# A planner that supposes a somewhat longer time for each fp32r matmul: a two-layer gated diffusion block on one core

## The chip, the core and the metric

The kernel runs on one core of a Trainium2 chip. The metric is the device time of one execution in microseconds (us), as a median of runs. A core has a matrix engine (TensorE, PE in the profile, with its weight loads as PEld), a vector engine (VectorE, DVE), a scalar engine (ScalarE, ACT), GpSimd (POOL) and SyncE (SP), which issues the DMA transfers here. Each engine takes its instructions in program order, and waits where an operand or a buffer is not ready.

## The reference, cut to what matters

512 latent tokens and 256 context tokens of width 1024 pass two layers (`DEPTH = 2`). In each layer the tokens are normed and modulated, projected to many parts by `w_in`, and go through four branches (a differential attention with 4 heads, a latent attention with 8 heads, a pooling mixer, a convolution); the branches are gated and merged, and a squared-ReLU MLP follows. In the second layer only the latent tokens are still needed behind the attention's keys and values.

```python
for l in range(DEPTH):
    px = split_in(modulate(rmsnorm(x, g_norm1[l]), mod_x[0], mod_x[1]) @ w_in[l])
    pc = split_in(modulate(rmsnorm(xc, g_norm1[l]), mod_c[0], mod_c[1]) @ w_in[l])
    ...
    ya_x = diff_post(attend(qa_x, ka_all, va_all, coef_a), g_sub_a[l], lam_init)
    yb_x = from_heads(attend(qb_x[None], kb_all[None], vb_all, coef_b))
    mix_x = merge_branches([ya_x, yb_x, pool_mixer(...), conv_mixer(...)],
                           px[10], w_branch[l], w_o[l])
    x = x + mod_x[2] * mix_x
    x = x + mod_x[5] * squared_relu_mlp(modulate(rmsnorm(x, g_norm2[l]), mod_x[3], mod_x[4]),
                                        w_ff1[l], w_ff2[l])
```

## The kernel before

**Arithmetic.** Every fp32 operand of a large product is split into a high and a low part of type fp32r (ACT makes the high part, DVE the low one), and each product is three matmuls: high x high, high x low, low x high. A weight block arrives by DMA in a raw buffer (`wr`), ACT writes `wh`, DVE writes `wl`, and PE multiplies into a PSUM tile (`mm`, and in the second layer's MLP also `mp`, `sp`, `pp`). Transposes through PE and a few true fp32 matmuls are the rest of PE's work.

**Stages.** For each layer: an attention stage (projections, both attentions, and beside them units of the gates, the pooling and the convolution), a merge stage, and an MLP stage. The second layer's MLP uses a seven-product scheme for part of its blocks.

**Who sets the order.** The program is not issued as it is written. Every instruction is recorded by `Plan.rec` with a cost from `Plan.cost`, into streams: B (the main line), A (an attention head), F (fill units: gates, pooling, convolution) and M (modulation work for later). `Plan.flush` gives each instruction of a stage a key: its stream's share of PE cost done so far, stretched over the whole stage's PE cost (M goes by DVE cost). `Plan.order` is a list scheduler: it simulates the five engines with these costs and with fixed hand-over times, and lets each engine take, of the instructions that are ready at its simulated time, the one with the lowest key. `Plan.replay` then emits the instructions in order of their simulated start, and pins that order per engine. Buffers of most kinds are handed out in recorded order, so the recorded order matters as well. It is set in part by `do_fill`, which is called at 37 places in layer 0 and 41 in layer 1 and records fill units of a list of 52 per layer for as long as the part of them recorded is below the part of the main line's PE cost `m / MAINPE[l]`.

The lines that matter in what follows:

```python
            if meth == 'transpose':
                return 109.0 if n > 64 else 60.0
            if ins[0].dtype == F32R:
                return n / 2.4 + 3 if n >= 256 else 4 * n / 2.4
...
            c = 0.833 * n + (52 if psum else 94)
...
                    lat = 0.0 if eng == 'SP' else (362.0 if je == 'PE' else 200.0 if je == 'ACT' or eng == 'PE' else 152.0)
...
            while fill and (nfill - len(fill)) < nfill * (m / MAINPE[l]):
```

They are the planner's charges for a PE transpose, for an fp32r matmul with n moving columns, for an ACT instruction with n columns, the hand-over time from one engine to another (`je` is the engine that waits), and the gate for fill units.

Of the kernel before, what the change touches and what calls it, by code (L numbers as in the profile page):

```python
# [33 lines left out]
HOLD = 0.85  # L34
TOG = (1, 0, 2, 1, 1)
FFLEAD = {'M': (0.1, 0.8)}
MAINPE = (327313, 279633)


class _Rec:  # L40
# [11 lines left out]
class Plan:  # L52
# [22 lines left out]
    def rec(self, eng, fn, meth, a, k):  # L75
        i = len(self.ops)
        ap0 = k['out'] if 'out' in k else a[0]
        outs = [ap0] + ([k['accum_out']] if k.get('accum_out') is not None else [])
        ins = [x for x in a[(0 if 'out' in k else 1):] if isinstance(x, bass.AP)]
        ins += [v for n, v in k.items() if n not in ('out', 'accum_out') and isinstance(v, bass.AP)]  # L80
        cost = self.cost(eng, meth, outs[0], ins, k)
        if eng == 'PE':
            self.pe += cost
        self.ops.append([eng, fn, a, k, cost, outs, ins])
        self.keys.append(0.0)
        self.phase.append(self.nphase)
        self.phase_ops.setdefault(self.stream, []).append(i)
# [30 lines left out]
    def cost(self, eng, meth, out, ins, k):  # L118
        n = self.free(out)
        if eng == 'PE':  # L120
            if meth == 'transpose':
                return 109.0 if n > 64 else 60.0
            if ins[0].dtype == F32R:
                return n / 2.4 + 3 if n >= 256 else 4 * n / 2.4
            return max(1000.0, 4 * n / 2.4)
        if eng == 'ACT':
            psum = any(x.space == bass.MemoryType.PSUM for x in ins[:1])
            c = 0.833 * n + (52 if psum else 94)
            c += 93.0 * (len(ins) - 1) + (93.0 if k.get('accum_out') is not None else 0)
            return c  # L130
        if eng == 'DVE':
            psum = any(x.space == bass.MemoryType.PSUM for x in ins) or out.space == bass.MemoryType.PSUM
            if meth == 'tensor_reduce':
                return 1.04 * self.free(ins[0]) + 69
            if meth == 'reciprocal':
                return 6.4 * n + 69
            if meth == 'tensor_tensor':
                return 1.04 * n + 69
            if meth == 'scalar_tensor_tensor':
                return 1.04 * n + 69 + 60 * (len(ins) - 2)  # L140
            return (1.04 if psum else 0.52) * n + 69 + 60 * (len(ins) - 1)
        if eng == 'POOL':
            return 1.0 * n + 80
        return 500.0
# [18 lines left out]
    def order(self):  # L163
# [3 lines left out]
        acc = {}  # L167
        tiles = {}
        for i, (eng, fn, a, k, cost, outs, ins) in enumerate(ops):
            touched = set()  # L170
            for w, aps in ((0, ins), (1, outs)):
# [55 lines left out]
        for i, (eng, fn, a, k, cost, outs, ins) in enumerate(ops):  # L227
            s = set(ap.tensor.name for ap in outs + ins if hasattr(ap.tensor, 'tag'))
            optiles[i] = [x for x in s if tiles[x][0] is not None]
# [134 lines left out]
def tile_block(ctx, tc, xT, ccol, wmod, cols, rows, wqkv, wcq, wckv, wuq, wukv, wpool,  # L364
# [825 lines left out]
    for l in range(DEPTH):  # L1190
# [30 lines left out]
        def do_fill():  # L1221
# [3 lines left out]
            s_, plan.stream = plan.stream, 'F'  # L1225
            while fill and (nfill - len(fill)) < nfill * (m / MAINPE[l]):
                fill.pop(0)()
# [398 lines left out]
```

## Time and profile before

| what | value |
|---|---|
| time before, median of 3 runs | 2667.26 us (2666.79 to 2670.55) |
| time of the profiled execution | 2668.45 us |
| span of the profiled execution (first to last instruction) | 2666.7 us |
| granted TensorE clock, mean | 0.999 of full |
| PE busy | 2630.7 us, 99% of the span |
| PEld busy | 2314.4 us, 87% |
| DVE busy | 1850.4 us, 69% |
| ACT busy | 1201.0 us, 45% |

Times in the rows are microseconds from the span's start; the mean of one instruction is in ns. A matmul's record reaches past the start of the next one, since matmuls are pipelined; how often one starts is read from the starts, not from the length of a record. All instructions carry line 352, since one helper emits them: groups are told apart by the names of their tiles.

### The profile page before, as it was taken

Reading aid. Unit: us, or ns where it says so; the run is one execution under the profiler, and the core shown is the slowest. Engines: PE = TensorE matmul, PEld = TensorE weight load, DVE = VectorE, ACT = ScalarE, POOL = GpSimd, SP = SyncE. Lnnn points to the kernel's source line nnn. Section 1 sums busy time; section 2 is a strip of 40 time slices with the busy share of each in tenths; the row PEclk is TensorE's granted clock in tenths of the full one; section 3 lists DMA queues with packets and bytes.
Section 4 is the critical chain, followed back from the end, with each engine's and each line's share of the span. In section 5 each row is a group of like instructions: output and inputs, shape, how many; then the busy total and the mean of one; then the engine's idle time right before and its main releaser. Section 6 shows DMA issues by size and latency. Waiting matters only on the chain.

```text
span 2666.7 us, 43004 instructions
## 1 busy us (share of the span) xinstructions
PE 2630.7 (99%) x15988; PEld 2314.4 (87%) x15988; DVE 1850.4 (69%) x4174; ACT 1201.0 (45%) x2488; POOL 13.7 (1%) x63
## 2 busy tenths in 40 slices
PE   8999999999999999999999999999999999999999
PEld 4898889988998888988888888888888888999988
DVE  6678666689986777445455467786467887887664
ACT  4355453445564135514141334555455562565443
POOL 0000000000000000000000000000000000000000
PEclk9999999999999999999999999999999999999999
DMA  7212233243446643333344323223232267433232
GB/s 246 77 62 70 85 109 114 94 125 118 129 135 198 216 134 105 103 97 109 114 136 127 121 95 100 68 68 106 93 98 83 90 182 225 149 109 107 84 103 95
DMA packets 189538, 311.97 MB, mean 117 GB/s; under 512 B 21520, under 2 KB 72080, under 8 KB 189328
## 3 DMA queue, kind: packets, MB, share of 16 engines
q1 hardware_dynamic: 189328, 309.22, 37.0%
q8 instruction: 126, 2.06, 0.3%
q14 instruction: 84, 0.69, 0.1%
HBM read 270.86 MB, written 38.27 MB: 116 GB/s over the span
## 4 chain that ended last, share of the span: by engine, by line
PE 92%; DMA 3%; DVE 3%; ACT 2%; issue 1%; SPq 0%; ACTq 0%; DVEq 0%
PE mm L352 75%; PE pst L352 8%; PE sc L352 5%; PE pp L352 2%; PE sp L352 1%; PE mp L352 1%; DMA wmp<-in_wmod_dram 1%; ACT wh L352 1%; DMA wr<-in_wff_dram 0%; DVE wl L352 0%; DMA wr<-in_wqkv_dram 0%; DMA gt<-g 0%; DMA wr<-in_wckv_dram 0%; DVE hl L352 0%; DVE e L352 0%
## 5 line engine op out<-in xcount | busy, mean ns | idle before, releaser
L352 ACT ACTIVATE wh<-wr 128x512 fp32r<-128x512 f32 (+3 forms) x616 | 367.1, 616 | 607.5 <-PE mm L352 453.4
L352 PE MATMUL mm<-hh,wh 128*128 128x512 f32 (+1 forms) x1792 | 539.5, 351 | 3.5 <-ACT gt L352 2.0
L352 PE MATMUL mm<-hh,wl 128*128 128x512 f32 (+1 forms) x1792 | 535.7, 349 | 0.8 <-DVE wl L352 0.8
L352 PE MATMUL mm<-hl,wh 128*128 128x512 f32 (+1 forms) x1792 | 533.1, 348 | 0.0
L352 DVE TENSOR_TENSOR wl<-wr,wh 128x512 fp32r<-128x512 f32 (+3 forms) x616 | 409.3, 673 | 132.4 <-ACT wh L352 118.6
L352 PEld LDWEIGHTS mm<-hh,wh 128*128 128x128 f32 x1792 | 333.9, 189 | 41.3 <-ACT gt L352 3.2
L352 PEld LDWEIGHTS mm<-hh,wl 128*128 128x128 f32 x1792 | 334.7, 189 | 39.5 <-DVE wl L352 1.1
L352 PEld LDWEIGHTS mm<-hl,wh 128*128 128x128 f32 x1792 | 334.1, 189 | 37.9
L352 DVE SCALAR_TENSOR_TENSOR macc<-wm,silu,macc 128x256 f32<-128x256 f32 x448 | 204.9, 479 | 96.2 <-DMA wm<-in_wmod_dram 90.2
L352 PE MATMUL mm<-ah,wh 128*128 128x512 f32 (+1 forms) x768 | 242.6, 356 | 0.4 <-ACT wh L352 0.3
L352 PE MATMUL mm<-al,wh 128*128 128x512 f32 (+1 forms) x768 | 242.1, 356 | 0.0
L352 PE MATMUL mm<-ah,wl 128*128 128x512 f32 (+1 forms) x768 | 241.7, 356 | 0.0
L352 ACT ACTIVATE ph<-pst 128x384 fp32r<-128x384 f32 (+1 forms) x216 | 102.9, 476 | 138.4 <-PE pst L352 136.6
L352 PEld LDWEIGHTS mm<-ah,wh 128*128 128x128 f32 x768 | 144.6, 188 | 22.1 <-ACT wh L352 0.8
L352 PEld LDWEIGHTS mm<-al,wh 128*128 128x128 f32 x768 | 144.6, 189 | 21.0 <-issue 0.2
L352 PEld LDWEIGHTS mm<-ah,wl 128*128 128x128 f32 x768 | 144.4, 188 | 21.1 <-issue 0.2
L352 ACT ACTIVATE e<-sc,st 128x768 f32<-128x768 f32 (+1 forms) x160 | 130.2, 814 | 67.5 <-DVE st L352 36.6
L352 PE MATMUL mm<-wh,hh 128*128 128x256 f32 x544 | 154.0, 287 | 2.2 <-ACT wh L352 1.1
L352 PE MATMUL mm<-wl,hh 128*128 128x256 f32 x544 | 155.0, 287 | 0.9 <-DVE wl L352 0.9
L352 PE MATMUL mm<-wh,hl 128*128 128x256 f32 x544 | 154.2, 285 | 0.0
L352 DVE SCALAR_TENSOR_TENSOR xx<-mm,mod,xx 128x256 f32<-128x256 f32 (+1 forms) x96 | 61.3, 659 | 133.8 <-PE mm L352 133.6
L352 DVE TENSOR_REDUCE st<-sc 128x1 f32<-128x768 f32 (+1 forms) x160 | 135.3, 846 | 20.6 <-PE sc L352 18.7
(233 smaller groups left out, 5112.6 us busy)
## 6 DMA issues: line engine op xcount, KB each, us to landing
wr<-in_wff_dram SPq DMA_DIRECT2D x280, 256.0 KB, 3.0
wr<-in_wdense_dram SPq DMA_DIRECT2D x192, 256.0 KB, 3.1
wm<-in_wmod_dram SPq DMA_DIRECT2D x320, 128.0 KB, 2.3
wr<-in_wbr_dram SPq DMA_DIRECT2D x64, 256.0 KB, 3.4
wr<-in_wqkv_dram SPq DMA_DIRECT2D x48, 256.0 KB, 2.8
g<-gt SPq DMA_DIRECT2D x32, 384.0 KB, 2.6
gt<-g SPq DMA_DIRECT2D x32, 384.0 KB, 3.5
wr<-in_wo_dram SPq DMA_DIRECT2D x48, 256.0 KB, 3.1
```

The costliest lines, as they stand in the source:

```text
L352: ins = fn(*a, **k).ins
```

## The change

Two constants of the planner change; no instruction is added, removed or resized. An fp32r matmul with 256 or more moving columns is charged n/2.4 + 13 ns in place of n/2.4 + 3 ns, and the two totals of main-line PE cost that the fill gate divides by are raised.

```diff
-MAINPE = (327313, 279633)
+MAINPE = (348900, 297430)
...
             if ins[0].dtype == F32R:
-                return n / 2.4 + 3 if n >= 256 else 4 * n / 2.4
+                return n / 2.4 + 13 if n >= 256 else 4 * n / 2.4
```

## Rows read from the trace of the kernel before

**Rows 1.** The page's first part: busy us (share of the span), instructions.

```profile
span 2666.7 us, 43004 instructions
...
PE 2630.7 (99%) x15988; PEld 2314.4 (87%) x15988; DVE 1850.4 (69%) x4174; ACT 1201.0 (45%) x2488; POOL 13.7 (1%) x63
```

**Rows 2.** Windows by time: busy us of each engine, clock, DMA share, GB/s.

```profile
500.00:900.00 400.00, 397.09 (x2533) 356.31 (x2532) 332.75 (x853) 202.29 (x457) 0.17 (x3) 1.00 0.47 148
900.00:1300.00 400.00, 398.17 (x2283) 347.81 (x2282) 234.12 (x443) 136.77 (x245) 0.00 (x0) 1.00 0.37 114
```

**Rows 3.** Timeline of PE in two stretches: start, us, instructions merged.

```profile
2404.63 0.39 PE L352 MATMUL mm<-ah,wl 128*128 128x512 f32 x1
...
2408.26 0.39 PE L352 MATMUL mm<-ah,wh 128*128 128x512 f32 x1
...
2600.47 1.60 PE L352 MATMUL sp<-t,wsf 128*128 128x256 f32 x12
2601.91 0.28 PE L352 MATMUL pp<-hh,wsf 128*128 128x256 f32 x1
```

**Rows 4.** PE groups that are not fp32r matmuls: form, count, busy us, mean ns.

```profile
L352 PE MATMUL pst<-ident,e 128*128 128x128 f32 x624 | 103.8, 273 | 1.1 <-DVE pl L352 0.8
...
L352 PE MATMUL pst<-ident,tmp 128*96 128x128 f32 (+1 forms) x318 | 57.3, 274 | 3.5 <-DVE ql L352 2.5 <-DVE ks L352 0.5 <-DVE nw L352 0.2
...
L352 PE MATMUL mm<-wmp,silu 128*2 128x512 f32 x64 | 30.4, 626 | 7.2 <-DMA wmp<-in_wmod_dram 7.2
...
L352 PE MATMUL pst<-ident,macc 128*128 128x128 f32 x128 | 22.0, 272 | 0.0
...
L352 PE MATMUL pst<-ident,ob 128*128 128x128 f32 x80 | 14.7, 273 | 0.0
...
L352 PE MATMUL R<-e,ones 128*128 128x256 f32 (+1 forms) x16 | 6.0, 467 | 0.9 <-DVE e L352 0.8
...
L352 PE MATMUL pss<-ident,ss 128*128 128x128 f32 x22 | 3.6, 277 | 0.9 <-DVE ss L352 0.9
...
L352 PE MATMUL pst<-ident,mrow 2*128 2x2 f32 x16 | 1.6, 202 | 1.6 <-ACT mrow L352 1.6
```

**Rows 5.** PE's waits in layer 0's attention stage (100 to 860): total, times, longest.

```profile
PE mm L352 <- ACT gt L352: 2.1, 3, 1.1
PE sc L352 <- ACT e L352: 1.2, 2, 0.7
PE pst L352 <- DVE pl L352: 0.8, 1, 0.8
PE pst L352 <- DVE ks L352: 0.5, 2, 0.4
```

**Rows 6.** PE's waits in layer 1's attention stage (1590 to 2170).

```profile
PE mm L352 <- ACT gt L352: 2.4, 3, 1.3
PE pst L352 <- DVE ql L352: 1.5, 3, 0.9
PE sc L352 <- ACT e L352: 1.2, 1, 1.2
PE mm L352 <- ACT wh L352: 1.1, 3, 0.7
PE mm L352 <- ACT wgh L352: 1.0, 1, 1.0
PE mm L352 <- DVE wl L352: 0.9, 1, 0.9
PE mm L352 <- DVE va L352: 0.5, 1, 0.5
PE pst L352 <- DVE nw L352: 0.2, 1, 0.2
```

**Rows 7.** The chain of work around one wait of PE, in order of time.

```profile
2368.05 0.53 ACT wsf L352
2368.58 0.04 issue
2368.63 0.50 PE sp L352 x2
```

**Rows 8.** All waits: the longest of ACT, and the weight split's form.

```profile
ACT wh L352 <- PE mm L352: 453.4, 163, 7.3
...
L352 ACT ACTIVATE wsf<-wr 128x512 fp32r<-128x512 f32 x84 | 51.1, 628 | 99.1 <-PE mm L352 50.5 <-issue 20.3 <-PE sp L352 8.6
```

## The prediction

> **What bounds the kernel now.** I read the page's totals first. The reader is to see that PE is busy for 2630.7 of 2666.7 us and DVE for 69% [rows 1]: all the time that PE stands idle is 2666.7 - 2630.7 = 36.0 us. The windows by time say the same of single stages: in a stretch of attention (500 to 900) PE is busy 397 of 400 us although DVE is at 333, and in a stretch of merge and MLP (900 to 1300) 398 of 400 with DVE at 234; the granted clock is full in both [rows 2]. So PE's own work sets the end, and an order of instructions can only move the waits between it.
>
> Next come PE's waits. In the two attention stages, where the order has most to choose, they are 2.1 + 1.2 + 0.8 + 0.5 = 4.6 us in 8 waits [rows 5] and 2.4 + 1.5 + 1.2 + 1.1 + 1.0 + 0.9 + 0.5 + 0.2 = 8.8 us in 14 [rows 6]: 13.4 us in 22 waits. Elsewhere the waits that one can name are fixed by data: 7.2 us for the first transfers, 1.6 us for `mrow`, 0.9 and 0.8 us in a norm [rows 4]. What is left, 36.0 - 13.4 - 10.5 = 12.1 us, is spread over stage borders and the end.
>
> A wait costs more than its idle time. A 256-column record is 0.28 us long, while the twelve of `sp` start every (2601.91 - 2600.47)/12 = 0.120 us [rows 3]; so about 0.28 - 0.12 = 0.16 us of each wait is hidden below the record before it. The 22 waits then cost 13.4 + 22 x 0.16 = 16.9 us, or 0.77 us each.
>
> **The change part by part.** *The charge.* Of 15988 matmul records [rows 1], 624 + 318 + 128 + 80 + 22 + 16 = 1188 are transposes and 64 + 16 = 80 true fp32 [rows 4]; 14720 are fp32r matmuls, all of 256 columns or more, so the planner now supposes 14720 x 10 ns = 147 us more of PE time. On the chip nothing is added: the same 14720 matmuls run at the same pace, so the direct cost is zero, and no cover is needed for that, since no instruction exists.
>
> Which charge is nearer the chip? 256 columns cost 256/2.4 + 3 = 109.7 ns before and 119.7 after, and the chip starts one every 120 ns [rows 3]. 512 columns cost 216.3 before and 226.3 after, and the sixteen steps from 2404.63 to 2408.26 give 226.9 ns [rows 3]. So the old planner ran PE 147 us ahead of the chip, and the new one runs with it. The Trainium skill says otherwise ("TensorE: Matmul & The Clock Gate", section "Back-to-back issue gap"): at the full clock an isolated matmul starts N/2.4 + 2.5 ns behind the one before, which is nearly the old charge. By that page 256 columns would take 109 ns; the trace has 120, and the measurement decides.
>
> *What that does to the order.* A PE clock that ran fast made ACT and DVE look slow beside it: the plan saw PE run dry at places where it does not, and put other streams' work there. It also left slack: for each matmul planned between a request and its answer, the chip gave 10 ns more than the plan thought. With the new charge the plan sees about 5.5% (147/2667) more room for every other engine, so it should find fewer dry places; against that, the slack goes. How much slack remains without it? The split `wsf` is charged 0.833 x 512 + 94 = 520 ns and the hand-over to PE 362, together 882; the chip needs 628 [rows 8] and about 50 ns from the end of ACT's record to PE's start (2368.63 - 2368.58) [rows 7], together 678. So 204 ns of slack per such hop stay in the plan whatever a matmul is charged.
>
> Keys move little, as a stream's progress is a share of its own PE cost; within a stream, transposes (charged 109 as before) lose a little weight against matmuls. What moves is which instructions are ready when an engine picks.
>
> *The gate.* Counted from the loops, the main line records 2196 fp32r matmuls in layer 0 and 1880 in layer 1, so `m` grows by 21960 and 18800 by its end; MAINPE grows by 21587 and 17797. The differences, 373 of 348900 (0.1%) and 1003 of 297430 (0.3%), are 52 x 0.001 = 0.06 and 52 x 0.003 = 0.18 of a fill unit. In the middle the 256-column projections, which come first, rise by 9% and the whole by 6.5%, so a unit that stood just under its step is recorded one call earlier; the recorded order is otherwise the old one. Both edits of the gate I cost at nothing: what hides it is PE's full queue (ACT waits 453.4 us for `mm` buffers [rows 8], not PE for ACT); with that cover gone, a unit a call early would cost one wait of 0.77 us.
>
> No row shows a wait of the new order. Below, the bound is that all 13.4 us of attention waits go with their hidden part: -16.9 us. Above, that they come twice: +16.9 us. Nearest are today's waits themselves, which a new order mostly moves. I take a fifth of 13.4 us as gain, 2.7 us, a judgement: more room, and slack that survives.
>
> **The sum.** Profiled execution 2668.45 us (span 2666.7 and 1.75 around it), which is 1.2 above the median 2667.26. Work 0, waits -2.7: 2665.75, and 2664.6 beside the median.
>
> **The rivals.** *Same (forecast).* Waits change places; within 0.2% (5.3 us, about what a measurement of this kernel can tell from no change). 2664.6 us; own range 2662 to 2672.5.
>
> *Faster.* The true charge removes most waits that the old plan made by its mistake: 9 to 17 us of attention waits and borders, 2667.3 - 10 = 2657 us. For it: 22 short waits, each of one to a few matmuls' length [rows 5, 6], are what a plan with a wrong clock leaves. Against it: 13.4 us is all there is, and part of it (the first `ks`, `ql`) hangs on chains without filler.
>
> *Slower.* The lost slack decides: a softmax's way over DVE and ACT back to PE is now planned to the nanosecond, and a producer that is late on the chip (a DMA behind `wr`, another instruction ahead of it on DVE, which is at 83% in 500 to 900 [rows 2]) stops PE at once, and behind it all of PE's queue. It decides from 5.3/0.77 = 7 more waits than the 22. At 11 more: 11 x 0.77 = +8.5 us, 2676 us; at 22 more, 2684. For it: DVE's load, and that the plan pins PE's order. Against it: the 204 ns per hop.
>
> *The skill's pace.* If 2.5 ns were right, the new plan would run PE 147 us behind the chip and PE would come to every answer early, which is the slower case at its full price, 2684 us. Rows 3 speak against it; 0.02, inside the slower chance.
>
> *Nothing happens at all*, the order being the same: with 147 us of shift in 2667 hardly possible, and inside "same".
>
> **How the numbers follow.** Faster 0.32, same 0.43, slower 0.25. Predicted 2664.6. The range runs from 2654 (some 13 us, most of the attention's waits, gone) to 2679 (15 more waits, 11.6 us); about 0.1 is left out on each side.
>
> **What would show it.** Right: the same 15988 PE records and PE busy time within some us of 2630.7 where waits no longer hide; 0.120 and 0.227 us paces as before; PE's idle time, 36.0 us, down by 1 to 4; another order in the attention stages and nearly the old one in the MLPs. Wrong: idle time on PE up by over 5 us with waits for `e`, `pl` or `st` in the attention stages (slack lost), or down by over 5 us there (the old clock had cost more); or a time that moves with the MLP stages, where I expect nothing.

## The result, and the profile after

The changed kernel takes 2688.93 us (median of 4 runs, 2687.51 to 2690.88) against 2667.03 us for the kernel before (4 runs): a ratio of 1.008, 95% interval 1.0062 to 1.0097. It is slower by 21.9 us, outside the predicted range. The profiled execution took 2690.17 us, with a span of 2688.4.

The page's first part, of the changed kernel (busy us, share of the span, instructions):

```profile
span 2688.4 us, 42996 instructions
...
PE 2642.2 (98%) x15988; PEld 2316.2 (86%) x15988; DVE 1846.3 (69%) x4174; ACT 1203.0 (45%) x2488; POOL 13.4 (0%) x63
```

The span is 21.7 us longer than before [rows 1]. The same 15988 matmuls ran, PE stood idle for 2688.4 - 2642.2 = 46.2 us in place of 36.0 (10.2 more), and the other 11.5 us lie inside PE's busy time (2642.2 against 2630.7). DVE and ACT did the same instructions in nearly the same time.

Where the 11.5 us sit can be counted from the start of every PE record in the two traces. Stops of PE (idle time before a record, however short) rise from 63 to 91. The record before a stop reaches some 0.17 us past the pace, so 28 more stops put 5.1 us into busy time. The other 6.4 us are steps that take longer than the pace without any idle time, half of them among the six steps behind a stop. Few of the longer steps have the signal (semaphore) that the matmul waits for come inside them: they account for 5.1 us, against 4.0 before. So these 6.4 us are not shown to be short waits for another engine; what they are stays open.

The Trainium skill ("Perfetto Trace Analysis", section "Identifying the Most-Contended Engine") says that matmul busy time is not a good measure of how close a kernel is to the chip's limit, and points to the busy share of the weight loads beside another measure. Here too PE's busy time misleads: PEld is busy 1.8 us longer than before, PE 11.5, for the same instructions.

The pace of PE did not change. Timeline of PE, changed kernel, in the second layer's MLP (31 steps between these two records):

```profile
2422.83 0.39 PE L352 MATMUL mm<-ah,wl 128*128 128x512 f32 x1
...
2429.86 0.39 PE L352 MATMUL mm<-ah,wh 128*128 128x512 f32 x1
```

(2429.86 - 2422.83)/31 = 0.2268 us for 512 columns, as before (0.2269, [rows 3]) and nowhere near the 0.216 of the old charge.

The windows by time, changed kernel (length, then busy us of PE, PEld, DVE, ACT, POOL, clock, DMA share, GB/s):

```profile
500.00:900.00 400.00, 391.80 (x2485) 348.89 (x2484) 328.28 (x850) 199.39 (x456) 0.16 (x3) 1.00 0.44 141
900.00:1300.00 400.00, 398.77 (x2290) 348.73 (x2289) 236.97 (x443) 137.77 (x244) 0.00 (x0) 1.00 0.38 117
```

The stretch in attention lost (391.8 us busy and 2485 matmuls, against 397.1 and 2533 in [rows 2]); the one in merge and MLP did not (398.8 against 398.2); the clock is full in both. Where each stage ends says it more exactly. The first `mm<-mh,wh` matmul, the first product with the merged tokens, marks the end of a layer's attention and of nearly all its merge; the last `mm<-ah,wh` matmul of 256 columns marks the end of layer 0's MLP. Timeline of PE, kernel before:

```profile
967.38 0.40 PE L352 MATMUL mm<-mh,wh 128*128 128x512 f32 x1
...
1585.42 0.28 PE L352 MATMUL mm<-ah,wh 128*128 128x256 f32 x1
...
2269.95 0.28 PE L352 MATMUL mm<-mh,wh 128*128 128x256 f32 x1
```

Timeline of PE, changed kernel:

```profile
984.58 0.40 PE L352 MATMUL mm<-mh,wh 128*128 128x512 f32 x1
...
1600.42 0.28 PE L352 MATMUL mm<-ah,wh 128*128 128x256 f32 x1
...
2288.07 0.28 PE L352 MATMUL mm<-mh,wh 128*128 128x256 f32 x1
```

The delay is 984.58 - 967.38 = 17.2 us after layer 0's attention and merge, 1600.42 - 1585.42 = 15.0 after its MLP, 2288.07 - 2269.95 = 18.1 after layer 1's attention and merge, and 21.7 at the end. So layer 0's attention and merge carry most of it, layer 0's MLP wins back 2.2 us, layer 1's attention and merge lose 3.1, and the last MLP 3.6.

PE's waits in layer 0's attention stage, changed kernel, 100 to 870 (total us, times, longest):

```profile
PE pst L352 <- DVE pl L352: 3.7, 4, 1.4
PE pst L352 <- DVE e L352: 2.5, 2, 1.5
PE pst L352 <- DVE nw L352: 1.6, 1, 1.6
PE mm L352 <- ACT wh L352: 0.7, 1, 0.7
PE pst L352 <- DVE ql L352: 0.7, 2, 0.4
PE pst L352 <- DVE ks L352: 0.5, 2, 0.4
PE pst L352 <- ACT wh L352: 0.5, 1, 0.5
PE mm L352 <- ACT gt L352: 0.5, 1, 0.5
PE mm L352 <- DVE wl L352: 0.4, 1, 0.4
PE pst L352 <- DVE tmp L352: 0.4, 1, 0.4
PE mm L352 <- ACT tmp L352: 0.3, 1, 0.3
PE pst L352 <- DVE bql L352: 0.2, 1, 0.2
PE sc L352 <- ACT e L352: 0.2, 1, 0.2
```

They sum to 12.2 us in 19 waits, against 4.6 in 8 [rows 5], and what is waited for has changed: before mostly ACT, now DVE, for `pl`, `e`, `nw`. In layer 1's attention stage (1605 to 2190) they are 9.9 us in 19, against 8.8 in 14 [rows 6]. Before a transpose into a new `pst` tile may start, DVE must have read the old one (`pl`, `ql`, `ks`, `bql`); there is one such PSUM buffer for stream A and one for the others.

One of them in full. The chain of work around it, in order of time, changed kernel:

```profile
795.66 4.89 DMA tmp<-y
...
800.57 0.85 ACT yh L352
...
801.44 0.96 DVE yl L352
802.40 0.08 DVE nw L352
802.48 0.48 DVE pl L352
802.95 0.04 issue
803.00 0.55 PE pst L352 x3
```

A transfer lands late (4.89 us; the planner's charge for its 393216 bytes, on a free queue, is 500 + 650 + 393216/360 + 900 = 3142 ns). ACT and DVE hold their pinned orders: ACT stands before `yh` and DVE before `yl`, work of the merge stage, while `ph` and `pl`, the two readers of the transposes' buffer, are queued behind them. PE stops for 1.4 us at a transpose whose own operand `e` was long there.

### The profile page after: what moved, and what is told of

It reads as the page before. It is cut to its first block, busy times and chain, and to the rows that moved or that the text cites. A ratio compares the mean times of both kernels' runs of the same rounds, so it can differ in the third digit from the quotient of the medians.

```text
span 2688.4 us, 42996 instructions
## 1 busy us (share of the span) xinstructions
PE 2642.2 (98%) x15988; PEld 2316.2 (86%) x15988; DVE 1846.3 (69%) x4174; ACT 1203.0 (45%) x2488; POOL 13.4 (0%) x63
## 4 chain that ended last, share of the span: by engine, by line
PE 83%; DVE 8%; DMA 4%; ACT 3%; issue 1%; SPq 0%; ACTq 0%; DVEq 0%
PE mm L352 68%; PE pst L352 7%; PE sc L352 4%; PE pp L352 2%; DVE wl L352 1%; DVE e L352 1%; PE sp L352 1%; PE mp L352 1%; DMA wr<-in_wff_dram 1%; DMA wm<-in_wmod_dram 1%; DVE hl L352 1%; ACT wh L352 1%; DMA wmp<-in_wmod_dram 1%; DVE st L352 1%; DVE nw L352 1%
## 5 line engine op out<-in xcount | busy, mean ns | idle before, releaser
L352 DVE TENSOR_TENSOR wl<-wr,wh 128x512 fp32r<-128x512 f32 (+2 forms) x616 | 409.0, 672 | 112.5 <-ACT wh L352 97.3
```

The lines of the kernel that those rows point to most:

```text
L352: ins = fn(*a, **k).ins
```

## The experiments

Each is compared with runs of the kernel before on the same chip (medians 2667.2 to 2668.1 us).

**Charge or gate.** Run e1 keeps the new charge in the schedule and the old count in the gate, so that the recorded order is the old one.

```diff
-MAINPE = (348900, 297430)
+MAINPE = (327313, 279633)
...
-            self.pe += cost
+            self.pe += cost - (10.0 if meth == 'matmul' and ins[0].dtype == F32R else 0.0)
```

> Matmuls are charged n/2.4 + 13 in the schedule, but the fill gate counts with the old charge and the old totals, so the recorded order is that of the kernel before. Lost-slack theory: the schedule's charge is the cause, so 2683 to 2692 us, as the changed kernel. Gate theory (the few fill units that are recorded one call earlier shift the buffers' order): 2664 to 2671, as before. Lucky-draw theory (the old order was a lucky one, any new order costs some 20 us): anything from 2675 to 2695.

Measured: 2692.17 us, ratio 1.0094 (1.0077 to 1.0111). Run e2 is the reverse, the kernel before with `MAINPE = (348900, 297430)` and `+ (10.0 if ...)` in the gate's count.

> The schedule charges n/2.4 + 3 as before, the gate alone counts with the new charge and the new totals. Lost-slack theory: 2662 to 2673 us, near the kernel before. Gate theory: 2683 to 2692. Lucky-draw theory: clearly slower than before, 2675 or more, since many orders change with the recorded one.

Measured: 2669.05 us, ratio 1.0005 (0.9996 to 1.0015). The schedule's charge is the whole cause; the gate costs nothing that can be told, as predicted. That another recorded order costs nothing speaks against the lucky draw. These two pairs also tell how far two recorded orders differ under the same charge: 1.6 us here, 3.2 between e1 and the changed kernel. No other pair was tried, so differences of some 3 us between the runs below are not read as causes.

**Slack given back.** Run e3, the changed kernel with a later release of buffers in the plan:

```diff
-                    heapq.heappush(tagfree[tag], lastuse[nm_] + 150.0)
+                    heapq.heappush(tagfree[tag], lastuse[nm_] + 300.0)
```

> The changed kernel, but the planner supposes that a buffer comes free 300 ns behind its last use in place of 150. In the changed kernel's trace most of the new waits of PE are for a PSUM buffer that ACT or DVE has just read, with 54 to 147 ns from the end of that reader's record (itself some 80 ns longer than the planner's charge) to PE's start: 130 to 230 ns against the 150 planned. Lost-slack theory with the slack missing at the buffer hand-over: at least half of the 21.7 us comes back, 2678 us or less. Lost-slack theory with the slack missing in general (queues of DVE and ACT): 2680 to 2688. Lucky-draw theory: 2680 to 2695, no better than the changed kernel but by chance.

Measured: 2671.46 us, ratio 1.0017 (1.0007 to 1.0026): four fifths of the loss come back.

Run e4, the changed kernel with all else scaled:

```diff
+SCALE = 1.07
...
+        if not (eng == 'PE' and meth == 'matmul' and ins[0].dtype == F32R):
+            cost *= SCALE
...
-                dma_free = max(dma_free, fin + 650) + b / 360.0
-                fin = dma_free + 900
+                dma_free = max(dma_free, fin + 650 * SCALE) + b / 360.0 * SCALE
+                fin = dma_free + 900 * SCALE
...
-                if fin + lat > ready_t[j]:
-                    ready_t[j] = fin + lat
+                if fin + lat * SCALE > ready_t[j]:
+                    ready_t[j] = fin + lat * SCALE
...
-                    heapq.heappush(tagfree[tag], lastuse[nm_] + 150.0)
+                    heapq.heappush(tagfree[tag], lastuse[nm_] + 150.0 * SCALE)
```

> The changed kernel, with every other charge of the planner (DVE, ACT, POOL, transposes, true fp32 matmuls, DMA, hand-overs, buffer release) times 1.07, so that the ratio between fp32r matmuls and all else is about that of the kernel before (256 columns were 109.7 and are 119.7, a factor of 1.09; 512 columns 216.3 and 226.3, 1.05). Lost-slack theory: what counts is the ratio, so most comes back, 2664 to 2674 us. Lucky-draw theory: it is one more new order, 2675 to 2695.

Measured: 2664.19 us, ratio 0.9987 (0.9978 to 0.9997). All of it comes back. The page's first part, run e4:

```profile
span 2661.4 us, 42965 instructions
...
PE 2626.8 (99%) x15988; PEld 2312.5 (87%) x15988; DVE 1847.9 (69%) x4174; ACT 1200.6 (45%) x2488; POOL 13.4 (1%) x63
```

PE's idle time is 2661.4 - 2626.8 = 34.6 us, and its busy time fell by 15.4 us from the changed kernel's: both halves of the loss are gone. The charge as such did no harm; its ratio to the rest did.

Run e5, the changed kernel with more at each data hand-over:

```diff
-... (362.0 if je == 'PE' else 200.0 if je == 'ACT' or eng == 'PE' else 152.0)
+... (512.0 if je == 'PE' else 350.0 if je == 'ACT' or eng == 'PE' else 302.0)
```

> The changed kernel with 150 ns more at every hand-over of data from one engine to another (to PE 512 in place of 362, to ACT and from PE 350 in place of 200, the rest 302 in place of 152); buffers still come free 150 ns behind their last use. Theory that the slack is missing at the buffers alone, since data hand-overs to PE keep some 200 ns: little comes back, 2680 to 2690 us. Theory that slack anywhere on the way from PE over DVE and ACT back to PE serves (a longer planned way also ends later for the buffer's reader): at least half comes back, 2678 or less.

Measured: 2669.25 us, ratio 1.0007 (0.9997 to 1.0016). The buffers are not the only place: slack in the data hand-overs serves as well.

**Slack taken away.** Run e6, the kernel before with `lastuse[nm_] + 0.0` in place of 150.

> The kernel before (charge n/2.4 + 3) with a buffer planned free at once at its last use, 0 ns in place of 150. Theory of slack at the buffers: the old charge's slack is eaten up there and the time rises, 2675 us or more. Theory of slack in general: a smaller rise, 2668 to 2676. No effect, 2664 to 2670, would speak against buffers as the place.

Measured: 2700.92 us, ratio 1.0128 (1.0109 to 1.0147): 33.7 us lost without any change to the charge. Run e7, the changed kernel with `n / 2.4 + 23` and `MAINPE = (370487, 315227)`.

> Matmuls charged n/2.4 + 23, again 10 ns more, with the gate's totals raised by the same step once more. Lost-slack theory: the plan now runs PE some 150 us behind the chip, slack turns negative, and the loss grows on: 2700 to 2730 us. Theory that a right charge is best and 13 was merely an unlucky draw: no trend, 2670 to 2695.

Measured: 2735.65 us, ratio 1.0254 (1.0239 to 1.027), more than the highest figure expected. The page's first part and the longest of PE's waits, run e7:

```profile
span 2735.3 us, 43031 instructions
...
PE 2669.1 (98%) x15988; PEld 2310.3 (84%) x15988; DVE 1849.8 (68%) x4174; ACT 1204.1 (44%) x2488; POOL 13.7 (0%) x63
```

```profile
PE mm L352 <- DMA wmp<-in_wmod_dram: 7.9, 3, 5.0
PE sc L352 <- ACT e L352: 6.0, 10, 1.6
PE pst L352 <- DVE ql L352: 5.4, 7, 1.4
PE pst L352 <- DVE pl L352: 5.1, 10, 1.2
```

PE busy grew by 38 us over the kernel before with the same 15988 matmuls, and the waits for `e`, `ql` and `pl` are the longest in total behind the one for the first transfers: the same picture, enlarged. Run e9 goes the other way, the kernel before with `n / 2.4 - 7` and `MAINPE = (305726, 261836)`.

> Matmuls charged n/2.4 - 7, 10 ns less than in the kernel before, with the gate's totals lowered by the same step. The times so far are 2667 at 3, 2689 at 13 and 2736 at 23. If slack is still short at 3: 2655 to 2663 us. If enough slack is there at 3 (what waits are left are fixed by data or by dry places): flat, 2663 to 2672. If too much is lost to a plan that no longer resembles the chip: 2672 or more.

Measured: 2675.95 us, ratio 1.003 (1.0019 to 1.0042), the third of the cases. So of the four charges tried one in between is best: 2676 at -7, 2667 at 3, 2689 at 13, 2736 at 23. Its page's first part:

```profile
span 2674.1 us, 42976 instructions
...
PE 2627.9 (98%) x15988; PEld 2315.6 (87%) x15988; DVE 1838.1 (69%) x4174; ACT 1199.6 (45%) x2488; POOL 13.4 (1%) x63
```

Here the loss has another face: PE's idle time is 46.2 us, as long as the changed kernel's, but its busy time did not grow (2627.9): fewer and longer stops.

**Which stages, which hand-overs.** Run e10 charges 13 in the attention stages alone:

```diff
+        if self.mode != 'attn' and eng == 'PE' and meth == 'matmul' and ins[0].dtype == F32R:
+            cost -= 10.0
```

> The charge of n/2.4 + 13 in the two attention stages alone, n/2.4 + 3 in the merge and MLP stages and the start. If the attention's PSUM buffers are the place, as the traces say: 2680 to 2690 us. If the other stages share in it by more than a fifth: 2672 to 2682.

Measured: 2686.62 us, ratio 1.0072 (1.0055 to 1.0088): 2686.6 - 2667.8 = 18.8 us are lost with the charge there alone, of 21.9 with it everywhere. Run e12 is e3 for PSUM buffers alone, run e15 for buffers in SBUF alone:

```diff
+PSUM_TAGS = ('mm', 's', 'ptA', 'ptB')
...
-                    heapq.heappush(tagfree[tag], lastuse[nm_] + 150.0)
+                    heapq.heappush(tagfree[tag], lastuse[nm_] + (300.0 if tag.split('_')[0] in PSUM_TAGS else 150.0))
```

> The changed kernel with 300 ns in place of 150 for PSUM buffers alone (matmul, score and transpose tiles); buffers in SBUF come free after 150 ns as planned before. If PE's waits for PSUM tiles are the place: as with 300 ns for all buffers, 2667 to 2675 us. If buffers in SBUF (weights, exponentials) matter as much: 2676 to 2686.

> The changed kernel with 300 ns for buffers in SBUF and 150 for PSUM buffers, the other half of the run with 300 for all. If the two kinds add up: some 10 us come back, 2676 to 2682. If PSUM buffers gave what they gave only by chance of the order: 2668 to 2675 or 2684 and more.

Measured: 2681.21 us for PSUM, ratio 1.0051 (1.0036 to 1.0066), and 2680.64 us for SBUF, ratio 1.0045 (1.003 to 1.006): 7.7 and 8.3 of the changed kernel's 2688.9 us back, together 16.0 beside the 17.5 of e3. My theory that PSUM buffers were the place fell; both kinds serve alike. Run e13 raises only the hand-over to PE (362 to 512), run e14 only the others (200 to 350, 152 to 302).

> The changed kernel with 150 ns more on the hand-over to PE alone (512 in place of 362). In the traces the hand-over to PE takes 140 to 150 ns from the end of the planner's charge, so 210 ns are spare there already. Theory that a hop serves only where it is short: little comes back, 2680 to 2690 us. Theory that slack anywhere on the way round from PE to PE serves alike: half or more of what all hops gave, 2669 to 2679.

> The changed kernel with 150 ns more on the hand-overs to ACT and DVE and from PE (350 and 302 in place of 200 and 152), to PE 362 as before. In the traces these hops take 200 to 212 ns from PE and 145 from ACT to DVE: nothing is spare there. Theory that a hop serves where it is short: nearly all that all hops gave, 2667 to 2674 us. Theory that slack anywhere serves alike: about as the run with the hop to PE alone.

Measured: 2682.87 us for the one, ratio 1.0052 (1.0037 to 1.0067), 2678.11 us for the other, ratio 1.0033 (1.0023 to 1.0042): 6.1 and 10.8 us back, together 16.9 beside the 19.7 of e5. Neither theory is met whole: e13 lies where "a hop serves only where it is short" put it, e14 in neither range. The others serve more, but the hand-over to PE gives 6.1 us although it had slack to spare, which suggests that slack counts as a sum over the way round.

**Both kinds together, and on top of the scaling.** Run e11 joins e3 and e5, run e8 is e4 with `300.0 * SCALE` for buffers.

> The changed kernel with both kinds of slack, 150 ns more at each hand-over of data and 300 ns in place of 150 for a buffer. Each alone gave 2669 to 2671 us. If slack only has to be enough somewhere on the way: 2662 to 2670, no more than either. If the two add: 2655 to 2662, below the kernel before.

> All other charges times 1.07 as in the run before that did so, and a buffer planned free after 300 x 1.07 = 321 ns in place of 160. If slack is still short at the buffers: faster than that run, 2652 to 2662 us. If the slack there was enough: no gain, or a loss by dry places that the plan now sees, 2662 to 2672.

Measured: e11 2665.42 us, ratio 0.9993 (0.9984 to 1.0003); e8 2662.42 us, ratio 0.9983 (0.9973 to 0.9993). The second buffer margin of e8 gains nothing over e4 that can be told. Only e8 (by 4.8 us) and e4 (by 3.2) beat the kernel before with an interval that leaves out 1, and not by much. With more slack than that the time settles within 5 us of the kernel before.

## Why the prediction was wrong, point by point

**PE bounds, the pace stays, the work is nil: right.** 15988 matmuls at 0.2268 us for 512 columns, as before.

**Which charge is nearer the chip: right, and beside the point.** The trace bears out 13 (0.2268 us for 512 columns), and not the N/2.4 + 2.5 ns that the Trainium skill gives for an isolated matmul ("TensorE: Matmul & The Clock Gate", section "Back-to-back issue gap"). Yet the plan with 3 is the faster one. That a plan resembles the chip more closely in one number does not make its order better.

**The gate at nothing: right.** Run e2: +0.05%, interval -0.04% to +0.15%.

**"So 204 ns of slack per such hop stay in the plan whatever a matmul is charged": the step that failed.** The number was right for the hop that I took, from ACT's data to PE. But the hop to PE is the most generous one, and I took it for all. Timeline of ACT and DVE, changed kernel:

```profile
86.70 0.49 ACT L352 ACTIVATE qd<-pst 64x384 fp32r<-64x384 f32 x1 [0.62 <-DVE qd L352]
...
87.22 0.56 DVE L352 TENSOR_SCALAR qd<-pst 64x384 fp32r<-64x384 f32 x1 [0.55 <-ACT qd L352]
```

From the one's start to the other's are 0.52 us; the planner charges 0.833 x 384 + 52 = 372 and 152, together 524 ns. And the hand-over of a buffer from DVE to PE, in the same trace:

```profile
802.39 0.55 DVE L352 TENSOR_TENSOR pl<-pst,ph 128x384 fp32r<-128x384 f32 x1
...
803.00 0.55 PE L352 MATMUL pst<-ident,e 128*128 128x128 f32 x3 [1.37 <-DVE pl L352]
```

0.61 us, planned 1.04 x 384 + 69 = 468 and 150, together 618. Most such waits are longer, as here:

```profile
87.80 1.12 DVE L352 TENSOR_TENSOR ql<-pst,qd 64x384 fp32r<-64x384 f32 x2
...
89.07 0.52 PE L352 MATMUL pst<-ident,tmp 128*128 128x128 f32 x3 [1.23 <-DVE ql L352]
```

From the end of the second `ql` (87.80 + 1.12 = 88.92) to PE's start are 0.15 us, or 0.70 from the start of a 0.55 us record, against the 0.618 planned. Of the 20 waits of PE in this trace that DVE's read of a PSUM buffer ended (for `pl`, `ql`, `ks`, `bql`, `tf`), 14 are of this kind and 6 of the other. So on the way from ACT to DVE nothing is spare, and at the release of a buffer the plan is mostly some 0.08 us short. What the old plan had there, by my reading, was the 10 ns of each matmul planned meanwhile; without it a late transfer or a queue on DVE, as in the chain at 803, reaches PE in full. The runs show the slack from both sides: put back at the buffers (e3), in the hand-overs (e5) or in all else (e4) it restores most or all of the time, and taken from the old plan at the buffers (e6) it costs 33.7 us. That a single hop works in the way told here is argued from these records, not tested by itself.

**The sum, -2.7 us for more room and surviving slack: wrong in sign.** PE's idle time rose by 10.2 us, with waits for `pl` and `e` in the attention stage, which is the prediction's own sign of being wrong. What the fewer dry places gave was not measured by itself.

**The slower rival had the mechanism and a price somewhat too low.** It named the softmax's way over DVE, a producer late by a DMA or by another instruction ahead of it, and doubled waits. In the two attention stages the listed waits rose from 22 to 38, in the whole kernel from 40 to 62 (about 31 to 40 us; the lists leave out idle times below 0.15 us). For 22 more, at 0.77 us each, it reached 2684; the chip gave 2688.9, which is 21.9/22 = 1.0 us for each. The price held a wait's idle time and what the record before it hides; it did not hold the longer steps without idle time, 6.4 us here. Its chance, 0.25, leaned on the 204 ns.

**Places.** Attention as the place: right (e10, 18.8 us with the charge there alone). That the MLP stages stay put was wrong by some us each way: layer 0's won back 2.2 us, the last lost 3.6. The split between the layers is not fixed either: in e10's trace the delay is 14.8 us at the first marker, 12.4 after layer 0's MLP and 19.7 at the last marker, so layer 1's attention and merge lose 7.3 there, against 3.1 in the changed kernel. Why was not tried. Why a charge of n/2.4 - 7 costs 8.2 us is open too: its trace shows longer stops of PE, not their reason in the plan.

## What to carry to other kernels

In an order fixed ahead of time from a cost model, a charge that is too low on the bound engine can be the margin that hides errors in the other charges; before it is corrected, each hand-over should be checked for what the plan leaves spare, the tightest one first and buffer release included. Give the margin by name (here 150 ns more per data hand-over, or 7% on all else) when the charge is set right. About half of this loss stood in the bound engine's busy time, with the same instructions, so compare stage ends, not lists of waits alone.

## What the runs showed of the hardware

An fp32r matmul of 512 columns started every 0.2268 us and one of 256 every 0.120 us in an unbroken stream at a full granted clock (1.00), 13 ns above n/2.4 in both. Where PE waited for DVE's last read of a PSUM buffer, it started 0.06 us behind the end of DVE's record in 6 of 20 cases (802.39 + 0.55 to 803.00) and 0.15 us behind it in 14 (88.92 to 89.07).
